# Output projection of a decoder block in seven block products, its weight differences made by adding transfers

## The chip, the cores and the metric

One core of a Trainium2 chip. The metric is the device time of one execution in microseconds, given as the median of three runs. The five engines (TensorE, VectorE, ScalarE, GpSimd or POOL, and SyncE, whose queue issues transfers) each work through a queue of their own in order and meet at semaphores.

## The reference, cut to what matters

One decoder layer for 512 tokens of width 1024, all in float32:

```python
p = x @ W_in + b_in                     # u, v, q, k, value, r, gate A, gate B
m = sigmoid(g_a) * y_a + sigmoid(g_b) * y_b     # y_a: spatial gating; y_b: gated linear attention * silu(r)
h = layer_norm(ALPHA * x + m @ W_out, ln1_g, ln1_b)
f = square(relu(h @ W_1)) @ W_2                 # 1024 -> 4096 -> 1024
out = layer_norm(ALPHA * h + f, ln2_g, ln2_b)
```

The change concerns `m @ W_out` (512 x 1024 by 1024 x 1024), the layer norm behind it, and the last gates ahead of it.

## The kernel before

**Split operands.** TensorE multiplies in a reduced float32 format (`F32R`). Each operand is split into an upper and a lower half: `split(hi, lo, src)` casts on ScalarE (L88) and subtracts on VectorE (L89). Each product is three passes: hi*hi, hi*lo, lo*hi.

**Weights.** All weights come as chunks of 128 x 1024 values (512 KB) in the order of the list `STREAM`. `load_to` issues the transfers on SyncE's queue into three `raw` buffers, `sum_to` makes weight differences on VectorE (L128), and `split_to` splits a chunk into `wh`, `wl`; there are `W_BUFS = 7` pairs of them, and a split is emitted up to seven chunks ahead of its use. One job of the gate stage uses one chunk (24 matmuls of 512 columns, 8 row blocks times three passes).

**Stages.** (1) Input projections, interleaved with the linear attention and the spatial gating. (2) The gate stage: `branch(e0)` takes the columns of r and of gate B in pairs, four jobs a pair; at the end tile `e` of `AT_` holds m transposed (128 channels x 512 tokens), and is split into `mh`, `ml`. (3) The output projection: two `row_unit`s, one for each half of the columns, four token tiles each, 24 matmuls a tile (L218). `out_take` adds ALPHA * x (L871), takes statistics (L872), and after the second half normalises the tile by rows (`ln_apply`: L638 to L646, with a power on POOL, L176). `turn_h` transposes a normalised tile on TensorE (L851, eight matmuls) and splits it into `xh`, `xl`, the right-hand operand of the feed-forward. (4) The feed-forward. Its first block is cut into two halves of 256 tokens (`hidden`), so that it can start when tiles 0 and 1 are there; tiles 2 and 3 are turned after its groups 0 and 2. Its second matrix is multiplied for three quarters of its rows in *seven products* instead of eight (`product_of`, Winograd's form of Strassen's scheme over 2 x 2 blocks): sums and differences of blocks on both sides, `GOES` and `accumulators` saying which PSUM banks a product adds to. The banks `x` carry products 1, 6, 7 and 4 in turn, the banks `v` products 5 and 3; each sum that is read out goes into a 128 x 512 quarter of the result.

**What sets the order.** Tensor, vector, scalar and POOL instructions stand in the order in which the code emits them. SyncE's queue is ordered by the scheduler. So an instruction that waits holds up all that was emitted behind it on its engine.

## Time and profile before

| | |
|---|---|
| median of three runs | 757.26 us (756.94 to 757.44) |
| the profiled execution | 757.19 us, span 755.4 us |
| granted TensorE clock | 0.998 |
| busy | PE 746.2, VectorE 473.8, ScalarE 343.6, POOL 29.8 us |
| transfers | 85.14 MB, 113 GB/s on average |

In the profile's rows, PE is TensorE's matmuls, PEld its weight loads, DVE is VectorE, ACT ScalarE, SP SyncE. A row of the timeline gives start and duration in us, engine, line and operation, `out<-in` by the program's names, and in brackets the idle time before it with what ended it. A row of the groups gives the count, then the busy time, the mean ns of one, and the idle time before. Matmuls overlap: one lasts 0.39 us in its row but the next starts sooner, so their cost is read from start to start.

### The profile page before, as it was taken

The numbers are of one execution on the slowest core, as the hardware profiler recorded it, in microseconds if no ns is written. First come the engines' busy times: TensorE is split into PE (matmuls) and PEld (weight loads), VectorE is DVE, ScalarE is ACT, GpSimd is POOL, SyncE is SP. The second block draws the span as 40 slices with busy tenths as digits, with TensorE's granted clock in tenths as the row PEclk, the third lists the DMA queues.
The fourth block names the chain that finished last, engine by engine and source line by source line (L and its number), as shares of the span: only waits on it lengthen the run. The fifth ranks groups of instructions, "written<-read, shape, count | busy, mean of one in ns | idle before, by whom it ended". The sixth has DMA issues, their size and how long they took to land.

```text
span 755.4 us, 8781 instructions
## 1 busy us (share of the span) xinstructions
PE 746.2 (99%) x3498; PEld 626.0 (83%) x3498; DVE 473.8 (63%) x592; ACT 343.6 (45%) x449; POOL 29.8 (4%) x60
## 2 busy tenths in 40 slices
PE   9999999999999999999999999999999999999996
PEld 7878888888888888888888988888888888888885
DVE  7478876676575554435458533777667856687655
ACT  7375744363254735444222544444444554455300
POOL 1000000000000102000002000000000000000001
PEclk9999999999999999999999999999999999999999
DMA  8533322222042132432240324145331734135111
GB/s 341 203 134 125 132 82 80 84 84 84 31 145 77 56 126 84 170 109 85 98 152 31 109 72 147 49 134 201 111 112 34 244 100 152 56 125 196 43 56 56
DMA packets 25464, 85.14 MB, mean 113 GB/s; under 512 B 3088, under 2 KB 3344, under 8 KB 25424
## 3 DMA queue, kind: packets, MB, share of 16 engines
q1 hardware_dynamic: 25280, 84.33, 32.3%
q8 instruction: 27, 0.44, 0.2%
q10 hardware_dynamic: 144, 0.26, 0.1%
q14 instruction: 13, 0.11, 0.0%
HBM read 82.48 MB, written 2.10 MB: 112 GB/s over the span
## 4 chain that ended last, share of the span: by engine, by line
PE 96%; issue 1%; DVE 1%; DMA 1%; POOL 0%; DVEq 0%; POOLq 0%
PE f L691 22%; PE ps L218 17%; PE mx L974 9%; PE f L1074 6%; PE gb L691 6%; PE r L691 6%; PE ga L691 6%; PE u L691 6%; PE mv L974 4%; PE qk L691 3%; PE first L275 3%; PE m L974 2%; PE sc L519 2%; PE pm L744 1%; PE po L553 1%
## 5 line engine op out<-in xcount | busy, mean ns | idle before, releaser
L89 DVE TENSOR_TENSOR wl<-raw,wh 128x1024 fp32r<-128x1024 f32 x141 | 171.1, 1222 | 114.4 <-ACT wh L88 112.6
L88 ACT CAST wh<-raw 128x1024 fp32r<-128x1024 f32 x141 | 145.7, 1044 | 48.7 <-PE ps L218 23.7
L691 PE MATMUL f<-xh,wh 128*128 128x512 f32 (+1 forms) x288 | 105.4, 366 | 0.0
L691 PE MATMUL f<-xl,wh 128*128 128x512 f32 (+1 forms) x288 | 105.3, 365 | 0.0
L691 PE MATMUL f<-xh,wl 128*128 128x512 f32 (+1 forms) x288 | 105.2, 365 | 0.0
L691 PEld LDWEIGHTS f<-xl,wh 128*128 128x128 f32 x288 | 54.3, 189 | 8.8
L691 PEld LDWEIGHTS f<-xh,wl 128*128 128x128 f32 x288 | 54.3, 189 | 8.7
L691 PEld LDWEIGHTS f<-xh,wh 128*128 128x128 f32 x288 | 54.3, 189 | 8.7
L914 ACT ACTIVATE F<-f 128x512 f32<-128x512 f32 (+1 forms) x28 | 15.0, 537 | 80.2 <-PE f L691 79.1
L218 PE MATMUL ps<-wh,xh 128*128 128x512 f32 x128 | 50.4, 394 | 0.0
L218 PE MATMUL ps<-wh,xl 128*128 128x512 f32 x128 | 49.8, 389 | 0.0
L218 PE MATMUL ps<-wl,xh 128*128 128x512 f32 x128 | 49.8, 389 | 0.0
L974 PE MATMUL mx<-wh,oh 128*128 128x512 f32 x96 | 37.3, 389 | 0.0
L974 PE MATMUL mx<-wl,oh 128*128 128x512 f32 x96 | 37.3, 389 | 0.0
L974 PE MATMUL mx<-wh,ol 128*128 128x512 f32 x96 | 37.3, 389 | 0.0
L128 DVE TENSOR_TENSOR raw<-raw,raw 128x1024 f32<-128x1024 f32 x24 | 29.2, 1218 | 2.6 <-DMA raw<-in_w_all 2.6
L218 PEld LDWEIGHTS ps<-wh,xl 128*128 128x128 f32 x128 | 24.0, 188 | 5.0
L218 PEld LDWEIGHTS ps<-wl,xh 128*128 128x128 f32 x128 | 24.0, 188 | 4.9
L218 PEld LDWEIGHTS ps<-wh,xh 128*128 128x128 f32 x128 | 24.0, 188 | 4.8
L691 PE MATMUL u<-xh,wh 128*128 128x512 f32 x64 | 25.9, 405 | 0.0
L691 PE MATMUL ga<-xh,wh 128*128 128x512 f32 x64 | 25.9, 404 | 0.0
L88 ACT CAST oh<-d 128x1024 fp32r<-128x1024 f32 x12 | 12.6, 1051 | 29.1 <-DVE d L947 29.1
(242 smaller groups left out, 1557.4 us busy)
## 6 DMA issues: line engine op xcount, KB each, us to landing
raw<-in_w_all SPq DMA_DIRECT2D x136, 512.0 KB, 3.4
bufB<-in_head SPq DMA_DIRECT2D x4, 512.0 KB, 8.0
xr<-in_x SPq DMA_DIRECT2D x8, 256.0 KB, 3.5
out<-bufA SPq DMA_DIRECT2D x8, 256.0 KB, 2.0
bufA<-in_head SPq DMA_DIRECT2D x3, 512.0 KB, 5.6
brow<-in_b_in SPq DMA_DIRECT2D x4, 256.0 KB, 6.2
g<-in_ln_g SPq DMA_DIRECT2D x2, 512.0 KB, 5.9
b<-in_ln_b SPq DMA_DIRECT2D x2, 512.0 KB, 5.5
```

What stands on the lines that cost most here:

```text
L88: nc.scalar.copy(hi, src)
L89: nc.vector.tensor_tensor(lo, src, hi.bitcast(F32), op=ALU.subtract)
L128: nc.vector.tensor_tensor(raw, x_, y_, op=ALU.subtract)
L218: nc.tensor.matmul(ps, s_, m_, start=(k == 0 and i == 0), stop=(k == KT - 1 and i == 2))
L275: nc.tensor.matmul(first[e], s_, m_[:, k, :], start=(k == 0 and i == 0), stop=(k == KT - 1 and i == 2))
L519: nc.tensor.matmul(sc[:, c, 0:192], pr.kt[:, jc * P : (jc + 1) * P], pr.qt[:, jc, :], start=True, stop=True)
L553: nc.tensor.matmul(po, pr.AT[:, j, c, :], vs, start=True, stop=(c == 0))
L691: nc.tensor.matmul(ps, s_, m_, start=(k == 0 and i == 0), stop=(k == KT - 1 and i == 2))
L744: nc.tensor.matmul(pm[:, c, :], bufB[:, c, gs], wst[:, g, :], start=True, stop=True)
L914: nc.scalar.activation(dst, ps, AF.Relu)
L974: nc.tensor.matmul(ps, s_, m_, start=(begins and k == 0 and i == 0), stop=(k == 3 and i == 2), skip_group_check=True,)
L1074: nc.tensor.matmul(ps, s_, m_, start=(f == 0 and i == 0), stop=(f == 7 and i == 2))
```

## The change

The output projection is done in seven products of 24 matmuls with 512 columns (`product_of`, moved up from the feed-forward), in the order 1, 2, 5, 6, 3, 7, 4. Its left operands are made in the gate stage: `as_it_is(k, m)` splits a block of m, `summed(k)` makes the four sums and differences on VectorE and splits them. The gate tiles are taken in the pairs `PAIRED`, so that block row k of both column blocks is there together. The weight differences aren't subtracted on VectorE: after the split of a chunk ScalarE negates it in place, and a transfer issued by POOL adds the next chunk from memory to it (eight times: chunks 56, 57, 60 to 65, whose sums become chunks 60 to 63 and 66 to 69).

The layer norm behind it is done in three ways. Tile 0: `rest_of_stats` and `normalise` (ScalarE, by a row's scale and bias, without gain and offset), the transposes, and then gain and offset by columns on ScalarE in PSUM; its rows get gain and offset later, in the second feed-forward block. Tiles 1, 2 and 3: by rows on VectorE as before, with the gain rows loaded into the buffers of product 1's operand.

```diff
+PAIRED = ((0, 1), (4, 5), (2, 6), (3, 7))
@@ split_to
             if raw is not None:
                 split(hi, lo, raw)
+            if i in NEXT_BY_DMA:
+                nc.scalar.mul(raw, raw, -1.0)
+                nc.gpsimd.dma_start(raw, w_all[STREAM[NEXT_BY_DMA[i]][4]], accum_op=ALU.add)
@@ product_of: also for the output projection
-                    split_to(u0 + k // 2 + 1 + W_BUFS)
+                    split_to(u0 + k // 2 + 1 + ahead)
@@ gate stage
-    for e in range(2, KT, 2):
-        branch(e)
+    def as_it_is(k, m):
+        e, i = {1: (k, 0), 2: (k + 4, 0), 4: (k + 4, 1)}[m]
+        hi, lo = mf if m == 1 else (mh[:, MADE[m]], ml[:, MADE[m]])
+        split(hi[:, k, :], lo[:, k, :], AT_[:, e, i * 256 : i * 256 + 256])
+    def summed(k):
+        a = lambda i, j: AT_[:, k + 4 * (j - 1), (i - 1) * 256 : i * 256]
+        d = [temp(f"ms{k}_{i}").rearrange("p (m t) -> p m t", m=2) for i in range(2)]
+        (s1, s2), (s4, s3) = [(x_[:, 0, :], x_[:, 1, :]) for x_ in d]
+        nc.vector.tensor_tensor(s1, a(2, 1), a(2, 2), op=ALU.add)
+        for o, x_, y_ in ((s2, s1, a(1, 1)), (s4, a(1, 2), s2), (s3, a(2, 1), a(1, 1))):
+            nc.vector.tensor_tensor(o, x_, y_, op=ALU.subtract)
+        for i in range(2):
+            split(mh[:, 2 * i : 2 * i + 2, k, :], ml[:, 2 * i : 2 * i + 2, k, :], d[i])
+    branch(PAIRED[1], {4: all_of(0), 5: all_of(1)})
+    branch(PAIRED[2], {6: all_of(2)})
+    branch(PAIRED[3], {3: all_of(3)[:1], 7: all_of(3)[1:]})
@@ output projection
-    row_unit(mh, ml, out_take(0))
-    at(S_O + 5, lambda: turn_h(0))
-    at(S_O + 6, lambda: turn_h(1))
-    row_unit(mh, ml, out_take(1))
+    def normalise(t):
+        row = bufA[:, t, :]
+        nc.scalar.activation(row, row, AF.Identity, bias=rs1[t][:, 1:2], scale=rs1[t][:, 0:1])
+    def turn_h(t):
...
+            for i in range(4 if t == 0 else 0):
+                e = half * 4 + i
+                g_, b_ = ln1c[:, e : e + 1], ln1c[:, 8 + e : 9 + e]
+                nc.scalar.activation(pt[:, i, :], pt[:, i, :], AF.Identity, bias=b_, scale=g_)
...
+    def project_take(m, t, ps):
+        i, j = GOES[m]
+        dst, tt = quarter(bufA, i, j)[:, t, :], 2 * i + t
+        if m in NEW:
+            xr = mpool.tile([P, 512], F32, name=f"xr{m}_{t}", tag="xr", bufs=2)
+            nc.sync.dma_start(xr, x[tt * P : (tt + 1) * P, j * 512 : j * 512 + 512])
+            nc.vector.scalar_tensor_tensor(dst, xr, ALPHA, ps, op0=ALU.mult, op1=ALU.add)
+        else:
+            nc.vector.tensor_add(dst, dst, ps)
+        if m in (2, 3, 7, 4):
+            stats(tt, j)
+        if m == 3 and t == 0:
+            rest_of_stats(0)
+        elif m in (3, 4):
+            if m == 3:
+                normalise(0)
+            st = st1[tt].rearrange("p a b -> p (a b)")
+            ln_apply(bufA[:, tt, :], bufA[:, tt, :], st, *rows1["gb"], lnp, f"l1{tt}")
+        if m == 7 and t == 0:
+            turn_h(0)
+        if m == 4:
+            if t == 0:
+                turn_h(1)
+    for m in ORDER:
+        ahead = {3: W_BUFS - 2, 7: W_BUFS - 2, 4: W_BUFS - 3}.get(m, W_BUFS)
+        product_of(f"o{m}", m, mf if m == 1 else (mh[:, MADE[m]], ml[:, MADE[m]]), project_take, ahead)
+        if m == 2:
+            rows1["gb"] = [row_bcast(mpool, a, D, f"mf{i}") for i, a in enumerate((ln1_g, ln1_b))]
@@ second feed-forward block, after its first job
+            nc.vector.tensor_mul(bufA[:, t, :], bufA[:, t, :], g1)
+            nc.vector.tensor_add(bufA[:, t, :], bufA[:, t, :], b1)
@@ the stream of chunks
+        if p < 0 and m in (5, 6, 7, 4):
+            place = {5: b(1, 2), 6: b(2, 2), 7: b(1, 2), 4: b(2, 1)}[m]
+            return (None, None, B if m == 7 else A, p, place)
+        if p < 0 and m == 3:
+            return (b(2, 2), B, B, p, None)
```

Three places of the queues follow. In the names, the number behind `wh`, `wl` or `raw` is the chunk, `mxo1_0` is a PSUM bank of the products (`x` bank, half 0), `mo2` one of product 2, `mvo5` a `v` bank, and `xr6_0` the x tile for product 6, half 0. In the rows before, `ps_60_2` is the PSUM bank of the second column half's token tile 2.

ScalarE, from the last gate job on, before:

```order
L815 ACTIVATE gb7_2809<-gb7_2784,cols_sb_101 128x512
L88 CAST wh62_2813<-raw62_2707 128x1024
L88 CAST mh_2359<-bufA_91 128x512
L88 CAST wh63_2920<-raw63_2745 128x1024
L88 CAST wh64_2932<-raw64_2780 128x1024
L88 CAST wh65_2944<-raw65_2817 128x1024
L88 CAST wh66_2960<-raw66_2924 128x1024
```

and now, from the casts of the last operand row on:

```order
L90 CAST mh_2357<-ms3_0_2859 128x2x256
L90 CAST mh_2357<-ms3_1_2860 128x2x256
L90 CAST mh_2357<-bufA_91 128x256
L90 CAST wh63_2899<-raw57_2441 128x1024
L154 ACTIVATE raw57_2441<-raw57_2441 128x1024
L90 CAST wh64_2911<-raw64_2743 128x1024
L154 ACTIVATE raw64_2743<-raw64_2743 128x1024
L90 CAST wh65_2942<-raw65_2783 128x1024
L154 ACTIVATE raw65_2783<-raw65_2783 128x1024
L90 CAST wh66_2956<-raw64_2743 128x1024
L90 CAST wh67_2991<-raw65_2783 128x1024
```

A negation (L154) stands between the casts of chunks 63, 64 and 65, and the casts of 66 and 67 read what the adding transfers leave.

VectorE, in the middle of the projection, before (first column half):

```order
L871 SCALAR_TENSOR_TENSOR bufA_91<-xr0_2_2909,ps_56_2_2884 128x512
L872 BN_STATS st1_2_2342<-bufA_91 128x6
L89 TENSOR_TENSOR wl63_2921<-raw63_2745,wh63_2920 128x1024
L89 TENSOR_TENSOR wl64_2933<-raw64_2780,wh64_2932 128x1024
L89 TENSOR_TENSOR wl65_2945<-raw65_2817,wh65_2944 128x1024
L871 SCALAR_TENSOR_TENSOR bufA_91<-xr0_3_2956,ps_56_3_2913 128x512
```

and now, from product 2 to product 6:

```order
L91 TENSOR_TENSOR wl65_2943<-raw65_2783,wh65_2942 128x1024
L91 TENSOR_TENSOR wl66_2957<-raw64_2743,wh66_2956 128x1024
L970 TENSOR_TENSOR bufA_91<-bufA_91,mo2_1_2921 128x512
L939 BN_STATS st1_1_2341<-bufA_91 128x6
L968 SCALAR_TENSOR_TENSOR bufA_91<-xr5_0_2982,mvo5_0_2968 128x512
L91 TENSOR_TENSOR wl67_2992<-raw65_2783,wh67_2991 128x1024
L91 TENSOR_TENSOR wl68_3004<-raw56_2439,wh68_3003 128x1024
L968 SCALAR_TENSOR_TENSOR bufA_91<-xr5_1_3007,mvo5_1_2969 128x512
L968 SCALAR_TENSOR_TENSOR bufA_91<-xr6_0_3022,mxo1_0_2876 128x512
L91 TENSOR_TENSOR wl69_3032<-raw57_2441,wh69_3031 128x1024
L91 TENSOR_TENSOR wl70_3042<-raw70_2948,wh70_3041 128x1024
L968 SCALAR_TENSOR_TENSOR bufA_91<-xr6_1_3047,mxo1_1_2877 128x512
```

The sums that free PSUM banks (L968, L970) now stand behind lower halves of weights that depend on the adding transfers.

VectorE, around the turn of tile 1, before:

```order
L640 SCALAR_TENSOR_TENSOR bufA_91<-bufA_91,mv_l11_3031,g1_2352 128x1024
L646 SCALAR_TENSOR_TENSOR bufA_91<-bufA_91,rs_l11_3032,b1_2354 128x1024
L89 TENSOR_TENSOR xl_90<-pturn_3038,xh_89 128x4x128
L89 TENSOR_TENSOR xl_90<-pturn_3045,xh_89 128x4x128
L871 SCALAR_TENSOR_TENSOR bufA_91<-xr1_2_3077,ps_60_2_3052 128x512
```

and now, from the statistics of tile 2 in product 4 on:

```order
L939 BN_STATS st1_2_2342<-bufA_91 128x6
L648 BN_AGGR mv_l12_3170<-st1_2_2342 128x2
L183 TENSOR_SCALAR rs_l12_3171<-mv_l12_3170 128x1
L650 SCALAR_TENSOR_TENSOR bufA_91<-bufA_91,mv_l12_3170,mf0_2964 128x1024
L656 SCALAR_TENSOR_TENSOR bufA_91<-bufA_91,rs_l12_3171,mf1_2966 128x1024
L91 TENSOR_TENSOR xl_90<-pturn_3177,xh_89 128x4x128
L91 TENSOR_TENSOR xl_90<-pturn_3184,xh_89 128x4x128
```

Before, the lower halves of a turned tile (`xl`) follow the normalisation of the tile after it (here tile 0's follow tile 1's, with a later projection unit still on TensorE). Now tile 1's follow the sum and the normalisation of tile 2, with half of product 4 and the feed-forward next on TensorE.

## Prediction

> **What bounds the kernel now.** I read the page's first lines, then the chain of waits in order of time, then the stretches (busy time by engine), then the rows of each engine around the output projection.

> ```profile
> span 755.4 us, 8781 instructions
> PE 746.2 (99%) x3498; PEld 626.0 (83%) x3498; DVE 473.8 (63%) x592; ACT 343.6 (45%) x449; POOL 29.8 (4%) x60
> GB/s 341 203 134 125 132 82 80 84 84 84 31 145 77 56 126 84 170 109 85 98 152 31 109 72 147 49 134 201 111 112 34 244 100 152 56 125 196 43 56 56
> ```
> TensorE (PE) is busy all the time; VectorE (DVE), ScalarE (ACT) and the transfers only matter where they make it wait.

> ```profile
> 268.00:368.00 100.00, 100.00 (x459) 83.07 (x458) 43.73 (x54) 46.31 (x71) 6.50 (x16) 1.00 0.33 113
> 368.00:420.00 52.00, 52.00 (x269) 44.50 (x268) 35.52 (x47) 13.39 (x18) 6.08 (x4) 1.00 0.32 107
> ```
> Columns: PE, weight loads, DVE, ACT, POOL, granted clock, DMA share, GB/s. In the gate stage (268 to 368) both helpers are under half busy. In the projection (368 to 420) VectorE already works 35.5 of 52 us, ScalarE 13.4.

> ```profile
> 367.49 32.64 PE ps L218 x144
> 400.13 0.87 PE pturn L851 x8
> 401.00 5.47 PE ps L218 x24
> 422.34 1.25 PE pturn L851 x8
> 423.59 47.06 PE f L691 x264
> ```
> Read off: 32.64/144 = 0.2267 us for a 512-column matmul, 0.87 us for one token tile's eight transposes. After 423.6 TensorE runs unbroken, so a shift at the start of the feed-forward carries to the end.

> ```profile
> 367.32 0.39 PE L218 MATMUL ps<-wh,mh 128*128 128x512 f32 x1
> 412.63 0.28 PE L691 MATMUL f<-xh,wh 128*128 128x256 f32 x1
> 426.51 0.38 ACT L914 ACTIVATE F<-f 128x256 f32<-128x256 f32 x1 [2.29 <-PE f L691]
> 429.39 0.38 ACT L914 ACTIVATE F<-f 128x256 f32<-128x256 f32 x1 [2.05 <-PE f L691]
> ```
> The window that changes starts with the first projection matmul (367.32) and ends with the fourth group of the half-width feed-forward, 0.2 us before its relu at 426.51: 426.3. Groups of 24 are 429.39 - 426.51 = 2.88 us apart. Work in the window: 192 x 0.2267 + 4 x 2.88 + 4 x 0.87 = 58.5 of 59.0 us; about 0.5 us is waiting.

> **The change, priced.** *Removed:* 24 of 192 matmuls, 5.44 us of TensorE. A product is then two halves of 2.72 us.

> *VectorE's prices in the window:*

> ```profile
> 406.50 0.69 DVE L871 SCALAR_TENSOR_TENSOR bufA<-xr,ps 128x512 f32<-128x512 f32 x1 [0.37 <-PE ps L218]
> 407.22 0.69 DVE L872 BATCH_NORM_STATS2 st<-bufA 128x6 f32<-128x512 f32 x1
> 407.95 0.21 DVE L638 BATCH_NORM_AGGREGATE mv_l<-st 128x2 f32<-128x12 f32 x1
> 408.20 0.16 DVE L173 TENSOR_SCALAR rs_l<-mv_l 128x1 f32<-128x1 f32 x1
> 408.27 1.28 DVE L640 SCALAR_TENSOR_TENSOR bufA<-bufA,mv_l,g 128x1024 f32<-128x1024 f32 x1
> 409.99 1.28 DVE L646 SCALAR_TENSOR_TENSOR bufA<-bufA,rs_l,b 128x1024 f32<-128x1024 f32 x1 [0.44 <-POOL rs_l L176]
> 411.19 1.28 DVE L89 TENSOR_TENSOR xl<-pturn,xh 128x512 fp32r<-128x512 f32 x2
> 412.39 3.48 DVE L89 TENSOR_TENSOR wl<-raw,wh 128x1024 fp32r<-128x1024 f32 x3
> 415.79 0.68 DVE L871 SCALAR_TENSOR_TENSOR bufA<-xr,ps 128x512 f32<-128x512 f32 x1
> 408.43 1.52 POOL L176 TENSOR_TENSOR rs_l<-rs_l,nhalf 128x1 f32<-128x1 f32 x1 [4.82 <-DVE rs_l L173]
> L176 POOL TENSOR_TENSOR ss<-ss,nhalf 128x1 f32<-128x1 f32 x16 | 8.8, 548 | 1.3
> ```
> From start to start: a sum out of PSUM 0.61 (0.72 if the next needs it), statistics 0.73, the rest of a tile's normalisation 3.24 (407.95 to 411.19), a lower half `xl` 0.60, a weight's lower half `wl` 1.13. The power on POOL takes 1.52 beside a VectorE operation with two SBUF operands, 0.55 elsewhere.

> *ScalarE's prices:*

> ```profile
> 367.52 0.69 ACT L815 ACTIVATE gb<-gb,cols_sb 128x512 f32<-128x512 f32 x1 [2.65 <-PE gb L691]
> 385.25 1.05 ACT L88 CAST wh<-raw 128x1024 fp32r<-128x1024 f32 x1 [14.93 <-PE ps L218]
> L450 ACT ACTIVATE kt<-kt 128x1024 f32<-128x1024 f32 x6 | 6.4, 1062 | 9.1 <-DVE kt L436 9.1
> L673 ACT ACTIVATE bufB<-bufB,rs_sg 128x1024 f32<-128x1024 f32 x4 | 4.9, 1232 | 0.0
> L290 ACT CAST als<-als 128x128 fp32r<-128x128 f32 x2 | 0.5, 296 | 0.0
> L580 ACT ACTIVATE bufB<-po,ss 128x256 f32<-128x256 f32 x16 | 6.8, 471 | 0.2 <-POOL ss L176 0.2
> L480 DVE TENSOR_TENSOR dr<-dr,k 128x256 f32<-128x256 f32 x4 | 1.7, 425 | 0.1
> ```
> A negation costs 1.06 (the 128x1024 activation with a constant scale), the row normalisation of tile 0 1.23. A 128x128 scaling by columns has no row: between 0.30 (a cast of that size) and 0.47 (256 columns with a scale column); 0.37 taken, in the middle, as both differ by one step. Now ScalarE idles 14.9 us before 385.25; that room goes.

> *Operands in the gate stage:* per row of blocks four 128x256 sums (0.43), two splits of 128x512 and three of 128x256 replace two of 128x512. That is about 3 us more of VectorE for each of four rows, beside 56 us idle in 268 to 368, and four PSUM banks let TensorE run ahead: nothing. Only the last row can show: its first operand is done at 367.2 and wanted at 369.4, its second at 372.7 and wanted at 374.8. Without that cover the first products wait. The new order of the gate tiles moves whole 5.44 us jobs: nothing.

> *Negations and adding transfers.* Eight negations on ScalarE, each waiting for VectorE's `wl` of the same chunk with later casts queued behind; eight transfers on POOL's queue, where only the powers stand behind them, later. The first two (wanted 20 us after issue) are free. The adding transfer is in no row.

> ```profile
> raw<-in_w_all SPq DMA_DIRECT2D x136, 512.0 KB, 3.4
> bufB<-in_head SPq DMA_DIRECT2D x4, 512.0 KB, 8.0
> DMA to landing us min/median/max: 2.5/3.5/4.9
> ```
> The last row is that of the x tiles. The adding transfer moves the same 512 KB and takes in the held 512 KB: 3.4 if the second stream is hidden, 3.4 + 512 KB at the page's best 341 GB/s (1.5) if not. Nearest is the plain chunk: I take 4.1; ends 3.4 and 8.0 (four heads queued). [...]

> *The path, step by step.* Last gate sigmoid 367.52; cast of chunk 62; VectorE multiplies, adds, makes its `wl` (370.8); negation to 371.9; ScalarE's casts of the last operand row follow, to 375.2. Then three rounds cast, `wl`, negation for 63, 64, 65, 1.05 + 1.22 + 1.06 + 0.2 each: negation of 64 ends 382.2, of 65 385.6. Their transfers land 386.3 and 389.7, and chunks 66 and 67 are cast behind them. Behind `wl66` stand, in VectorE's queue, two sums and a statistics; `wl67`, `wl68`, two sums, `wl69`, `wl70` and a sum follow, and only then the sums of product 3.
> 1. Product 3 (ideally 389.1) reuses the bank of product 5, whose first sum is read at 390.6: 1.6; its second half 0.4.
> 2. VectorE has idled 2.2 behind negation 63, 3.1 behind transfer 64, 0.5 for an x tile (3.5 us; SyncE's queue has two weight loads ahead of the second), and 0.5 in small gaps. So the first sum of product 3, ready at 392.2 on an undisturbed TensorE, starts at 398.0. Sum, statistics, aggregate: 399.8; POOL 0.55 + 0.27; ScalarE 1.23: tile 0 is normal at 402.0, transposes wanted at 399.2: 2.8. The 0.55 is taken because the next VectorE operation there reads PSUM; 1.52 would make this 3.8. [...]
> 3. VectorE normalises tile 1 by rows (to 404.5), product 7's first sum and statistics (405.8), tile 0's two `xl` behind eight scalings (8 x 0.41) and two casts (408.2), `wl71`, `wl72` (410.9), then the second sum of product 7 (411.5). The second half of product 4 adds into that bank and is wanted at 409.3: 2.2.
> 4. Statistics, then tile 2's sum and whole normalisation stand ahead of tile 1's `xl` in the queue: 417.5. The second matmul of the feed-forward wants it at 414.3: 3.2.

> Hidden: x tiles are eight before and after; gain and bias rows loaded once more (1 MB, DMA busy 0.32); tile 0's later multiply and add, 2.5 us of VectorE beside groups of 5.44 on TensorE. Cover gone: they would come on top.

> **Sum:** -5.44 + (1.6 + 0.4 + 2.8 + 2.2 + 3.2 = 10.2) - 0.5 (the waiting that is there now) = +4.3. The profiled execution took 757.19 us (755.4 span and 1.8 around it), 0.07 under the median: 761.5.

> **The rivals.** (a) *Faster.* If VectorE never idles behind negations and transfers, its queue has 15.7 us of work from 376.0 and reaches product 3's sum at 391.7, on time. From 392.2 it still has 18.1 us in a row before tile 1's first `xl` (410.3), wanted at 407.3, so 3.1 wait: -5.44 + 3.1 - 0.5 = -2.8, 754.4; without any wait 751.3. For it: VectorE idles 16 of 52 us now. Against it: the queue is in order, and a negation stands in front of the cast that VectorE needs. It decides at product 3's first sum: every microsecond it is late goes to the end one for one, and past 2.8 us late the kernel is slower. (b) *The adding transfer is slow.* Each microsecond over 4.1 adds one: 7 gives 764.4, 8.0 765.4, past 8.3 two for one, as two transfers then follow each other; 9 gives 767. For it: POOL makes this transfer, no row shows it; against: 0.32 busy share. (c) *They cancel:* half the lateness, within 1.5 us of 757.2. For it: my small gaps are rounded; against: the tail alone takes 3.1.

> **How the numbers follow.** A difference under 0.2% (1.5 us) can't be told from none. The forecast as worked out: 0.50; its own range goes from 759.3 (transfer 3.4, x tile 2.5, scaling 0.30) to 764.5 (x tile 4.9, scaling 0.47). Rival (b), above that: 0.12. Rival (c): 0.12. Rival (a): 0.26. Faster 0.26, same 0.12, slower 0.62. The range 753.5 to 766.5 takes in most of (a) and of (b) and leaves out some 0.07 below and 0.06 above.

> **What would show it.** Right: gaps on TensorE before product 3, before the transposes of tile 0 (released by ScalarE), before the second half of product 4 and at the second feed-forward matmul (both by VectorE), near 10 us in all; `wl66` and `wl67` waiting for casts that wait for the adding transfers; landing near 4 us. Wrong: TensorE without gaps between 389 and 418, VectorE at product 3's first sum by 394, or a wait in the gate stage or after 430, where I have none.

## The result, and the profile after

The changed kernel takes 767.35 us (median of 5 runs, 765.80 to 768.99), the kernel before 757.13 beside it (5 runs, 756.94 to 757.44): 1.0136 times as long, 95% interval 1.0123 to 1.0149. Slower was forecast, but by 4.3 us; it is 10.2, and 767.35 lies outside the range of 753.5 to 766.5.

The page of the changed kernel (its execution took 767.35 us), the lines that answer to those of before:

```profile
span 765.6 us, 8831 instructions
PE 745.0 (97%) x3474; PEld 624.7 (82%) x3474; DVE 494.4 (65%) x632; ACT 365.7 (48%) x484; POOL 36.1 (5%) x69
q0 software_dynamic: 1152, 4.19, 3.2%
raw<-in_w_all SPq DMA_DIRECT2D x134, 512.0 KB, 3.3
raw<-in_w_all POOLq DMA_DIRECT2D x8, 512.0 KB, 5.9
```

TensorE is 20.6 us short of the span; before it was 9.2. The last row is the adding transfer, 5.9 us in the median; q0 is POOL's queue (packets, MB, share of 16 engines). The same stretches as before, with the columns of the prediction's table:

```profile
268.00:368.00 100.00, 100.00 (x459) 83.11 (x458) 51.24 (x75) 53.38 (x85) 10.17 (x20) 1.00 0.35 106
368.00:420.00 52.00, 42.07 (x183) 33.77 (x181) 36.82 (x53) 24.42 (x34) 7.35 (x8) 0.93 0.66 172
```

In the gate stage the 7.5 us more of VectorE stay hidden. In the projection TensorE works 42.1 of 52 us, and the granted clock is no longer 1.00. TensorE's waits between 370 and 430 (engine, line, for whom; us in total, times, longest):

```profile
PE mvo L841 <- DVE bufA L968: 4.9, 1, 4.9
PE f L701 <- DVE xl L91: 2.8, 1, 2.8
PE mxo L841 <- DVE bufA L970: 2.0, 1, 2.0
PE pturn L954 <- ACT bufA L946: 1.9, 1, 1.9
```

These are the four places of the prediction. TensorE's rows at the first and the last:

```profile
394.00 0.76 PE L841 MATMUL mvo<-wh,mh 128*128 128x512 f32 x1 [4.92 <-DVE bufA L968]
394.57 0.63 PE L841 MATMUL mvo<-wl,mh 128*128 128x512 f32 x1
394.99 0.63 PE L841 MATMUL mvo<-wh,ml 128*128 128x512 f32 x1
395.42 0.63 PE L841 MATMUL mvo<-wh,mh 128*128 128x512 f32 x1
...
418.64 0.28 PE L701 MATMUL f<-xh,wh 128*128 128x256 f32 x1
421.76 0.39 PE L701 MATMUL f<-xl,wh 128*128 128x256 f32 x1 [2.85 <-DVE xl L91]
...
422.35 0.41 PE L701 MATMUL f<-xl,wh 128*128 128x256 f32 x1
422.57 0.41 PE L701 MATMUL f<-xh,wl 128*128 128x256 f32 x1
422.78 0.41 PE L701 MATMUL f<-xh,wh 128*128 128x256 f32 x1
```

Behind both gaps the matmuls come 0.427 us apart (394.99 to 395.42) instead of 0.227, and 0.213 instead of 0.12 in the half-width groups. TensorE's clock in stretches (busy, clock, DMA share, GB/s):

```profile
394.00:398.00 4.00, 4.00 (x10) 0.50 0.74 264
...
421.70:425.30 3.60, 3.54 (x17) 0.55 0.22 55
425.30:430.00 4.70, 4.70 (x42) 0.98 0.99 323
```

Ten matmuls at half speed cost 2.0 us, the seventeen and their neighbours 1.6. From start to start, less a matmul (or the transposes), the gaps are 5.07, 2.06, 2.19 and 3.00. The account of TensorE's time: the matmuls saved, the four gaps, the slow matmuls, less the waiting of before: -5.44 + 12.3 + 3.6 - 0.5 = +10.0, against 10.2 measured.

Where VectorE got late: the chain's steps of the transfer that makes chunk 66 from 64 and of the last x tile ahead of product 3's first sum; ScalarE's cast behind the first, then VectorE, at `wl66` and at that x tile:

```profile
382.21 7.36 DMA raw<-in_w_all
...
396.75 4.65 DMA xr<-in_x
```
```profile
389.64 1.04 ACT L90 CAST wh<-raw 128x1024 fp32r<-128x1024 f32 x1 [4.43 <-DMA raw<-in_w_all]
...
390.72 1.22 DVE L91 TENSOR_TENSOR wl<-raw,wh 128x1024 fp32r<-128x1024 f32 x1 [6.60 <-ACT wh L90]
...
401.50 0.69 DVE L968 SCALAR_TENSOR_TENSOR bufA<-xr,mxo 128x512 f32<-128x512 f32 x1 [1.57 <-DMA xr<-in_x]
402.10 0.68 DVE L970 TENSOR_TENSOR bufA<-bufA,mvo 128x512 f32<-128x512 f32 x1
```

The x tile is requested only when product 5's second sum (396.05 to 396.7) has freed one of the two `xr` buffers. So the last thing that product 3's first sum waits for is this transfer of 4.65 us, and it is so in the rows of the runs below, but for `plain_sp`'s, which name TensorE; no run changed the number of these buffers or the time of the request.

### The profile page after: what moved, and what is told of

Its sections match the earlier page's. It is cut to its first block, busy times and chain, and to the rows that moved or that the text cites. A ratio compares the mean times of both kernels' runs of the same rounds, so it can differ in the third digit from the quotient of the medians.

```text
span 765.6 us, 8831 instructions
## 1 busy us (share of the span) xinstructions
PE 745.0 (97%) x3474; PEld 624.7 (82%) x3474; DVE 494.4 (65%) x632; ACT 365.7 (48%) x484; POOL 36.1 (5%) x69
## 4 chain that ended last, share of the span: by engine, by line
PE 92%; DVE 3%; DMA 2%; issue 2%; ACT 1%; POOL 0%; DVEq 0%; POOLq 0%; ACTq 0%
PE f L701 23%; PE ps L228 11%; PE mx L841 9%; PE f L1137 6%; PE gb L701 6%; PE r L701 6%; PE ga L701 6%; PE u L701 6%; PE mv L841 4%; PE first L285 3%; PE qk L701 3%; PE m L841 2%; PE sc L529 2%; DMA raw<-in_w_all 1%; PE pm L754 1%
## 5 line engine op out<-in xcount | busy, mean ns | idle before, releaser
L91 DVE TENSOR_TENSOR wl<-raw,wh 128x1024 fp32r<-128x1024 f32 x147 | 178.3, 1223 | 118.8 <-ACT wh L90 117.2
L90 ACT CAST wh<-raw 128x1024 fp32r<-128x1024 f32 x147 | 151.3, 1043 | 31.3 <-DMA raw<-in_w_all 10.5
## 6 DMA issues: line engine op xcount, KB each, us to landing
raw<-in_w_all SPq DMA_DIRECT2D x134, 512.0 KB, 3.3
raw<-in_w_all POOLq DMA_DIRECT2D x8, 512.0 KB, 5.9
bufB<-in_head SPq DMA_DIRECT2D x4, 512.0 KB, 8.1
bufA<-in_head SPq DMA_DIRECT2D x3, 512.0 KB, 5.5
g<-in_ln_g SPq DMA_DIRECT2D x2, 512.0 KB, 6.1
```

Of the source, the lines that this page charges most:

```text
L90: nc.scalar.copy(hi, src)
L91: nc.vector.tensor_tensor(lo, src, hi.bitcast(F32), op=ALU.subtract)
```

## The experiments

**Theory T:** each gap is a loss of its own; the late transfers open the first, and gaps halve the clock. **Theory V:** VectorE's queue, in order, sets the start of the feed-forward; a gap or a slow stretch ahead of its next late operation costs nothing more. A rival to both: the order of the tail (tile 1's `xl` behind tile 2's normalisation) is the main cost.

### Why the adding transfer is slow

`plain_pool`: the adding taken out, all else kept.

```diff
-                nc.gpsimd.dma_start(raw, w_all[...], accum_op=ALU.add)
+                nc.gpsimd.dma_start(raw, w_all[...])
```

> POOL's eight transfers write over the held chunk instead of adding to it (the weight differences are left out; negations, queue and bytes are the same). If the adding makes them slow (accumulate): landing near the plain 3.3 us, gap before product 3 down by 3 to 4 us to 1 to 2, its clock loss gone: 761 to 763 us. If it is POOL's queue or other transfers beside them: landing stays at 6 to 7.5 us, 766 to 768 us.

765.01 us. The page, POOL's transfers and TensorE's waits:

```profile
q0 software_dynamic: 1152, 4.19, 1.6%
raw<-in_w_all POOLq DMA_DIRECT2D x8, 512.0 KB, 3.6
```
```profile
PE pturn L954 <- ACT bufA L946: 3.5, 1, 3.5
PE f L701 <- DVE xl L91: 2.9, 1, 2.9
PE mvo L841 <- DVE bufA L968: 1.6, 1, 1.6
PE mxo L841 <- DVE bufA L970: 1.0, 1, 1.0
```

It is the adding: with the same packets and bytes the 16 engines are busy for 1.6% of the span instead of 3.2%, 1.5 us a transfer instead of 3.1 (765.6 x 0.032 / 8). The eight land after 3.4, 3.6 and 4.0 us (least, median, most) against 5.0, 5.9 and 9.2. In the changed kernel the four early ones land after 5.0 to 5.6, the one requested at 372.03, beside the gain and bias rows, after 9.2, and the three late ones after 6.1, 7.4 and 6.5. But the time fell by 2.3, not by 4 to 6: the gap before product 3 shrank by 3.3, the one before the transposes grew by 1.6.

`rows`: the request of the gain and bias rows stands later in the program.

```diff
-        if m == 2:
+        if m == 5:
             rows1["gb"] = [...]
```

> The gain and bias rows (1 MB, 5.8 and 8.9 us) are requested after product 5 in the program instead of after product 2, so that they no longer move beside the adding transfers of chunks 66 and 67. If the sharing of the DMA engines makes these slow: they land in 4 to 5 us, the gap before product 3 falls to 2 to 3 us, its clock loss goes in part: 762 to 765 us. If the transfer is slow by itself: 7.4 and 6.6 us as before, 766 to 768 us. If the rows now land too late for tile 1's normalisation, that shows as VectorE waiting for mf, and the time rises.

766.11 us, but nothing moved: SyncE, whose queue the scheduler orders, requests the rows at 373.09, 5.41 us behind the projection's first matmul, and in the changed kernel at 372.57, 5.41 behind it too. So this is the changed kernel once more. It says nothing of the rows, and shows that two medians of one order of work can lie 1.2 us apart. What the changed kernel's trace shows: both rows (5.8 and 8.9 us) have landed by 381.9, before the deciding transfer is requested at 382.21, so they don't share the engines with it; whether they push back the adding transfers ahead of it stays open. In the changed kernel:

```profile
378.00:384.00 6.00, 6.00 (x28) 4.95 (x28) 4.22 (x5) 3.56 (x4) 1.75 (x2) 1.00 1.04 272
384.00:389.00 5.00, 5.00 (x23) 3.88 (x21) 0.12 (x1) 1.06 (x1) 0.88 (x1) 1.00 1.00 188
```

The DMA share (last but one) is full, at 188 GB/s: three adding transfers, 3.3 us apart, need 3.1 us of all engines each. In `plain_pool`, with the same rows and x tiles beside it, the share is 0.60 in both stretches. In `rows` and `sub6` this transfer landed after 7.38 and 7.45 us. What it costs isn't fixed: in `late_d4`, which makes it too, product 3 waited 3.3 us instead of 4.9.

`sub6` was meant to take away the late pair; the expectation names the wrong chunks. Product 6 uses 62 and 63, made early, and the late ones, 66 and 67, are product 7's. So it is the control for the early pair:

```diff
-        if p < 0 and m in (5, 6, 7, 4):
+        if p < 0 and m in (5, 7, 4):
...
-        if p < 0 and m == 3:
-            return (b(2, 2), B, B, p, None)
```

> Product 6's two differences (chunks 66 and 67) are made on VectorE from a chunk loaded in the ordinary way; the other six stay negations with adding transfers. Theory T (the late adding transfers of 66 and 67, 7.4 and 6.6 us, hold ScalarE's and then VectorE's queue; the gap before product 3 follows from them, and TensorE's halved clock follows from that gap): the gap of 5.07 us before product 3 and its 2.0 us of clock loss go, the gap of 2.06 before tile 0's transposes shrinks to 0 to 1, the tail's gap stays or grows by 0 to 2: 757 to 760 us. Rival R2 (VectorE is too full for its queue whatever the transfers do, and gets 2.4 us more work here): product 3 still waits 3 us or more, 765 us or above.

767.27 us: to make the early pair's differences on VectorE instead gains nothing, which fits the prediction's nothing for them. `sub7` takes away the right pair (and its subtraction is b(1,2) less b(2,2), made by VectorE):

```diff
+        if p < 0 and m == 7:
+            return (b(1, 2), None, B, p, (None, B))
```

> Product 7's two differences (chunks 66 and 67, made from 64 and 65; the ones whose transfers took 7.4 and 6.6 us) are made on VectorE from plainly loaded chunks; their two negations and adding transfers go, the other six stay. Theory T (every microsecond by which those transfers are late goes to the end): gap before product 3 under 1 us, its clock loss gone, no other gap grows: 757 to 760 us. Theory V (VectorE's own queue, in order, sets the end of the stage; the late transfer only puts idle time into it): gap before product 3 under 1, but the sum of product 3 still comes at 397 to 399 instead of 402, and the gap before tile 0's transposes grows to 3.5 to 4.5 with a clock loss behind it: 763 to 765 us.

763.43 us, as V said. TensorE's waits:

```profile
PE pturn L954 <- ACT bufA L946: 4.7, 1, 4.7
PE f L701 <- DVE xl L91: 2.9, 1, 2.9
PE mxo L841 <- DVE bufA L970: 0.5, 1, 0.5
PE mvo L841 <- DVE bufA L968: 0.4, 1, 0.4
```

4.5 us of gap went before product 3, and 2.8 came back before the transposes, since product 3's first sum came at 398.36; VectorE waited 2.5 us for its x tile there.

### What a gap is worth

`plain_sp`: no differences at all.

```diff
+        if p < 0:
+            return ({1: b(1, 1), 2: b(2, 1), 5: b(1, 2), 6: b(2, 2), ...}[m], None, None, None, None)
```

> All fourteen chunks of the projection's weights are loaded in the ordinary way by SyncE; there are no negations, no adding transfers and no differences of weights (these are left out). The prediction's rival (a) in pure form: VectorE never idles behind them. By its sum 754.4, with a clock loss of 1.5 behind a tail gap of 3 us 755 to 757 us: no gap before product 3, transposes' gap under 1.5. If VectorE's other work alone is too much for the stage: product 3's first sum after 396, transposes' gap over 2, 760 us or more.

759.65 us, between the two. Product 3's first sum comes at 395.57, by estimate behind an x tile: VectorE frees its buffer at 390.20 and reads it at 394.97, 4.77 us later, as at 396.73 and 401.50 in the changed kernel. Three waits stay:

```profile
PE pturn L954 <- ACT bufA L946: 2.1, 1, 2.1
PE mxo L841 <- DVE bufA L970: 2.0, 1, 2.0
PE f L701 <- DVE xl L91: 1.3, 1, 1.3
```

So the waits from product 3's sum on are 5.4 us, as much as the matmuls save, even with no weight difference. `fill3`, `fillf` and `fill` put matmuls that nothing reads into the gaps:

```diff
+        if m == 3:
+            fill(20)
...
+    def fill(n):          # into a bank that nothing reads
+        for i in range(n):
+            nc.tensor.matmul(ps, mh[:, 2, 0, 0:P], ml[:, 2:4, 0, :], start=True, stop=True)
...
+            if part == e == 0:
+                for _ in range(20):
+                    nc.tensor.matmul(ps[:, :256], hh[:, 0, 0:P], hh[:, 0, 0:256], start=True, stop=True)
```

> 20 matmuls of 512 columns into a spare PSUM bank stand before product 3 and 20 of 256 columns before the first feed-forward group: 4.5 and 2.4 us of work that nothing reads, inside the gaps of 5.07 and 3.0. If the halved clock comes from the gap, both halved stretches go. If the clock loss adds to the end wherever it lies (theory T): 2.0 and 1.55 less, 763.5 to 764 us. If VectorE's queue sets the transposes' time (theory V), the 2.0 turn into a longer gap there (2.1 to about 4) and only the last 1.55 are gained: 765.5 to 766 us. If the clock does not depend on the gap: half-speed rows stay, 767 us.

> Only the 20 matmuls of 512 columns before product 3 (4.5 us inside the gap of 5.07), nothing else changed. If the clock loss behind that gap (2.0 us) adds to the end: 765.3 us. By theory V the transposes wait for a sum that VectorE makes at 402 either way: the 2.0 become a longer gap there and the time stays at 766.5 to 768 us.

> Only the 20 matmuls of 256 columns before the first feed-forward group (2.4 us inside the gap of 3.0). No wait follows there, so by both theories the slow matmuls behind it (1.55 us) are a loss of their own: 765.5 to 766.2 us. If the time stays at 767.3, the clock loss is not on the path there either and the missing microseconds are elsewhere.

764.70, 767.69 and 765.22 us. Before product 3 nothing is gained, as V says: the slow matmuls of product 3 went, and the wait for the transposes grew from 1.9 to 4.1. Before the feed-forward 2.1 us are gained in the median, of runs from 763.76 to 767.29; the profiled execution is the slowest of them and shows no gain, since there the filling held the second matmul up by 1.0 us. Both together gain 2.65.

```profile
PE pturn L954 <- ACT bufA L946: 4.1, 1, 4.1
PE f L701 <- DVE xl L91: 2.9, 1, 2.9
PE mxo L841 <- DVE bufA L970: 0.4, 1, 0.4
```

These are `fill3`'s waits. What V says is then seen across all the kernels that keep the order of the tail. Starts in each profiled execution: VectorE's first sum of product 3, the second feed-forward matmul, their difference, and the rest of the span behind it:

| kernel | sum | matmul | difference | rest |
|---|---|---|---|---|
| changed | 402.10 | 421.76 | 19.66 | 343.84 |
| rows | 402.78 | 422.44 | 19.66 | 342.36 |
| sub6 | 403.19 | 422.84 | 19.65 | 342.36 |
| plain_pool | 398.87 | 418.97 | 20.10 | 343.83 |
| sub7 | 398.36 | 418.46 | 20.10 | 342.74 |
| fill | 400.92 | 421.04 | 20.12 | 342.36 |
| fill3 | 401.67 | 421.33 | 19.66 | 345.07 |
| fillf | 402.66 | 423.28 | 20.62 | 342.22 |
| subpool | 395.97 | 416.06 | 20.09 | 343.94 |
| plain_sp | 395.57 | 415.22 | 19.65 | 342.68 |

The sum moves over 7.6 us, the difference over 0.5, but for `fillf`, where the filling itself comes in between. The rest is 342.2 to 342.7 with the clock full behind the last gap, 343.8 to 343.9 with half speed for 3.4 us there, and 345.07 with half speed for 6.8 us (`fill3`).

`tail`: tile 1's lower halves ahead of tile 2's normalisation.

```diff
+        if m == 4 and t == 0:
+            turn_h(1)
         if m in (2, 3, 7, 4):
             stats(tt, j)
...
-        if m == 4:
-            if t == 0:
-                turn_h(1)
```

> Tile 1's transposes' lower halves (xl) stand ahead of tile 2's normalisation in VectorE's queue; nothing else moves. Theory T: the gap of 3.0 us at the second feed-forward matmul goes to under 0.5, and its clock loss of 1.55 with it, while tile 2's transposes may wait about 1: 763 to 764 us; the gap before product 3 stays at 5. Rival R1 (this order is the main cost of the change): 757 us or less. If the clock loss doesn't follow from the gap: 764 to 765 us with half-speed matmuls still after the start of the feed-forward.

762.89 us, 4.5 less, just under the 763 to 764 expected. The wait at the feed-forward and the slow matmuls behind it are gone, one of 0.5 at tile 2's transposes came. The rival that this order is the main cost asked for 757 or less from this move alone.

### Other ways to make the differences, and other orders

`subpool`: all eight differences subtracted on POOL, from plainly loaded chunks.

```diff
-                    nc.vector.tensor_tensor(raw, x_, y_, op=ALU.subtract)
+                    (nc.gpsimd if STREAM[i][3] < 0 else nc.vector).tensor_tensor(raw, x_, y_, op=ALU.subtract)
...
-        if p < 0 and m in (5, 6, 7, 4):
+        if p < 0 and m == 7:
+            return (b(1, 2), None, B, p, (None, B))
+        if False:
```

> All eight differences of the projection's weights are subtracted on POOL, which idles there, from plainly loaded chunks; no negations and no adding transfers. No run shows the price of a 128x1024 subtraction on POOL; VectorE's takes 1.22 us, and POOL's power took 1.52 instead of 0.55 beside a VectorE operation with two SBUF operands. If POOL gets each done in under 3 us and does not slow VectorE: as the kernel without differences, 755 to 759 us. If it waits for VectorE or slows it: the casts of chunks 66 and 67 wait for POOL, 760 to 767 us.

761.73 us. POOL's subtractions, and VectorE's two `wl` beside them, which take 2.8 us each instead of 1.2:

```profile
L135 POOL TENSOR_TENSOR raw<-raw,raw x4: 2401/2899/3397, 377.5 to 386.8; 128x1024 f32<-128x1024 f32 x4
```
```profile
385.59 5.66 DVE L91 TENSOR_TENSOR wl<-raw,wh 128x1024 fp32r<-128x1024 f32 x2 [1.47 <-ACT wh L90]
```

Even so product 3's first sum comes at 395.97, 6.1 earlier. `late_d` and `late_p` make the move of `tail` and put tile 0's transposes behind the whole of product 7, with adding transfers and with POOL's differences:

```diff
-        if m == 7 and t == 0:
+        if m == 7 and t == 1:
             turn_h(0)
```

> Adding transfers stay as changed. Tile 1's lower halves stand ahead of tile 2's normalisation (762.89 alone), and tile 0's transposes now stand behind the whole of product 7 instead of its first half, so the sum of its second half is ahead of tile 0's lower halves on VectorE. Theory T (each gap is a loss of its own): the gaps of 2.3 at the transposes and of 2.2 before product 4's second half go, nothing takes their place: 758 to 759 us. Theory V (VectorE's queue from product 3's first sum to tile 1's lower halves is about 16 us of work and sets the start of the feed-forward): both gaps go, and one of 3 to 4 us with a halved clock behind it comes back at the second feed-forward matmul: 761.5 to 763.5 us.

> The eight differences are subtracted on POOL (761.73 alone), and the two moves of the run beside it are made. By theory V the first sum of product 3 comes at 396, tile 1's lower halves 16 us behind it at 412, wanted at 407.5: one gap of 4 to 5 us before the feed-forward and 1.5 of halved clock: 757 to 759 us. By theory T 753 to 755 us.

760.75 and 756.35 us, both better than V said and worse than T said. `late_p` is the only kernel that isn't slower than before: 0.9990 times as long (0.9981 to 0.9999, 11 runs), less than the 0.2% that count. Its waits:

```profile
PE mxo L841 <- DVE bufA L970: 1.9, 1, 1.9
PE pturn L954 <- ACT bufA L946: 0.4, 1, 0.4
```

The wait at the feed-forward that V had put there didn't come: with the sums ahead VectorE no longer idles for tile 0's casts, and tile 1's lower halves begin 13.1 us behind product 3's first sum (396.27 to 409.40), not 16. Between the two kernels lie 4.4 us, the price in this order of the adding transfers over POOL's subtractions. The two moves alone take 6.6 us off the changed kernel, POOL's subtractions alone 5.6, both together 11.0: order and transfers weigh about the same, so the rival of the tail's order is half right once tile 0's transposes are moved too. More tries to shorten VectorE's queue:

```diff
@@ late_p2: tile 2 as tile 0
+        elif m == 4 and t == 0:
+            rest_of_stats(2)
+            normalise(2)
...
-            for i in range(4 if t == 0 else 0):
+            for i in range(4 if t % 2 == 0 else 0):
@@ late_p3: that, and
-        ahead = {3: W_BUFS - 2, 7: W_BUFS - 2, 4: W_BUFS - 3}
+        ahead = {3: W_BUFS - 2, 7: W_BUFS - 4, 4: W_BUFS - 3}
...
             turn_h(1)
+            split_to(73)
@@ late_p4: the edit of late_p3 without that of late_p2, and; late_d4: the same with adding transfers
+        if m == 4 or (m == 7 and t == 1):
+            tt = tt if m == 4 else 1
...
-            elif e in (0, 2):
-                turn_h(2 + e // 2)
+            elif e in (1, 2):
+                turn_h(1 + e)
```

> As the run with POOL's differences and both moves, and tile 2 is normalised as tile 0 is (mean and scale on ScalarE before the transposes, gain and bias by columns behind them, its row multiply and add later beside the feed-forward): 2.6 us less of VectorE behind tile 1's lower halves. By theory V the gap before the feed-forward stays and only a wait of tile 2's transposes goes: 0.5 to 1.5 us less than that run.

> As the run with tile 2 on ScalarE, and the splits of chunks 71 and 72 (two lower halves of 1.13 us on VectorE) stand behind tile 1's lower halves instead of ahead. By theory V these come 2.3 us earlier and the gap before the feed-forward falls to about 2 us, too short for the clock to fall: 753.5 to 756 us, faster than both kernels. If VectorE's queue is not the bound there: no difference to the run with tile 2 on ScalarE.

> POOL's differences and both moves (756.35), and VectorE's order is changed again: both sums of product 7 stand ahead of tile 1's normalisation, the lower halves of chunks 71 and 72 behind tile 1's, and the transposes of tiles 2 and 3 come one and one half-width group later. By theory V the gap of 2.1 before product 4 goes, 1 to 3 us of small waits remain at the feed-forward's start: 753.5 to 756 us. If each wait only moves on: 756 to 757 us.

> The same order as that kernel with the eight negations and adding transfers of the change. What is left between the two is what the adding transfers cost once the order behind them is repaired: product 3's first sum at 401 instead of 396, so 4 to 5 us more, 758 to 761 us. If the order was all that mattered: within 1.5 us of the kernel with POOL's differences.

761.64, 763.63, 758.00 and 763.40 us: four misses; of the last the difference comes near (5.4 us for the adding transfers, 4 to 5 expected). `late_p4` lost the wait before product 4 for which it was made and got another; in `late_p2` and `late_p3` the wait at the feed-forward that they were to leave or to shorten was not there, and tile 3's transposes began to wait. The 2 us that `late_p3`'s expectation calls too short for the clock to fall are those of the changed kernel, where gaps of 2.06 and 2.19 left it at 1.00; in `late_p` it fell behind one of 2.13 (400.44 to 403.44, less the transposes). In `late_p2` tile 2's columns, scaled in PSUM on ScalarE (1.8 us and a cast for each bank, by the rows of `late_p3`), hold the banks that tile 3's transposes want; in `late_p4` tile 3's wait for tile 2's split. One line of each, `late_p2` first:

```profile
PE pturn L954 <- DVE xl L91: 3.7, 2, 2.0
```
```profile
PE pturn L954 <- DVE xl L91: 2.9, 1, 2.9
```

## Why the prediction was wrong

Right: the direction; the place and the releaser of each of the four gaps; the last three gaps' sizes within 0.8 us (2.06, 2.19, 3.00 against 2.8, 2.2, 3.2; the 2.06 in part by luck, as VectorE was 4.1 us later there than predicted and TensorE 5.1, by 3.1 more of the first gap and 2.0 of slow matmuls); the early transfers and the gate stage at nothing; the negation's price (1.06); the power's 0.55 in tile 0's chain (0.56 beside a sum out of PSUM, and 1.51 for tile 1's beside a VectorE operation with two SBUF operands, begun 0.16 us ahead of it). In the kernel before, two powers took 0.55 even though such an operation began beside them, 0.06 and 0.21 us behind their start (300.76 and 256.41). VectorE's queue from product 3's first sum to the second feed-forward matmul was worked out at 19.5 us and took 19.66.

Wrong, in three terms:
1. *The adding transfer*, taken at 4.1 from ends of 3.4 and 8.0. Issued at 382.21, when the prediction had the negation end (382.2), it landed after 7.36. The four early ones took 5.0 to 5.6, over the 4.9 that the prediction's estimate gives for a held chunk whose stream isn't hidden, and the three in a row, with the engines full (share 1.04 and 1.00), 6.1 to 7.4. The ends of 3.4 and 8.0 took it in, the value chosen between them was too low; rival (b), one microsecond for each over 4.1, gives 764.8 for it.
2. *The x tiles*: 0.5 predicted, 0.24 + 1.57 measured, 1.3 more. With both, product 3's first sum should come 4.6 late; it came at 402.10 instead of 398.0, 4.1.
3. *The clock*, which the prediction left out, and so put at nothing: half-speed matmuls cost 3.6 us, of which 2.0 are taken up by the next wait for VectorE (`fill3` gains nothing) and 1.6 count, as nothing waits behind them (the rest is 343.84 instead of 342.36).

With these the profiled execution comes to 761.5 + 4.1 + 1.6 = 767.2. `plain_pool`, where the deciding transfer took 4.03, is the prediction's own premise: it took 765.0, 3.5 over, of which 0.9 are a later sum, 0.6 a longer queue behind it (20.10) and 1.5 the clock; the rest lies between its profiled execution (764.6) and the median. So the transfer alone isn't the miss. One sum of the prediction doesn't come out either: its own range's upper end, 764.5, is 0.8 more than the two terms named for it give (1.4 and 8 x 0.10 over 761.5); a transfer of 4.9 would make that up.

Rival (a) said 754.4 if VectorE never idles behind negations and transfers. `plain_sp` is that and took 759.65. The rival's queue, which was to reach product 3's sum at 391.7, on time, reached it at 395.57, 3.4 after the 392.2 at which the prediction has its first half ready: by the same estimate the x tile again. Behind it come not one wait of 3.1 but three, 5.9 in all from start to start, and the queue to the second matmul is 19.65 instead of 18.1. The 3.4 and the 1.6 make up 5.0 of the 5.3 us. Its turning point (slower past 2.8 us late) put this kernel on the right side: it is 1.0036 times as long as before (1.0024 to 1.0049).

## What to carry to other kernels

When one engine's queue sets the end of a stage, follow its time to the next fixed point; a gap closed on the engine that waits came back here at the next place where it meets that queue (with `fill3` 1.9 us before the transposes became 4.1). An adding transfer kept the DMA engines busy twice as long as a plain one of the same bytes (3.1 us against 1.5), and three of them 3.3 us apart filled the engines and landed after 6.1 to 7.4 us instead of 5.0 to 5.6, though the pair wanted 20 us later cost nothing (`sub6`). Look in the trace whether an edit moved the request that it was to move. Half speed followed waits on TensorE of 1.9 (`late_p`) to 4.9 us here and didn't follow others of 1.9 and 2.0 (the changed kernel, before the transposes and product 4): after a predicted gap of that size price a stretch of half-speed matmuls (1.6 and 2.0 us here), and ask whether another wait comes before the end that takes it up.

## What the runs showed of the hardware

```profile
409.23 0.54 PE L841 MATMUL mxo<-wh,mh 128*128 128x512 f32 x1 [2.02 <-DVE bufA L970]
...
409.99 0.63 PE L841 MATMUL mxo<-wh,ml 128*128 128x512 f32 x1
410.42 0.63 PE L841 MATMUL mxo<-wh,mh 128*128 128x512 f32 x1
```

The two slow stretches of the changed kernel begin 30.72 us apart, nine times 3.413. In `fillf`, `late_p3`, `late_p2` and `late_d4` the edges of two slow stretches, read off the spacing of the matmuls, lie six, seven, eight and ten times 3.413 us apart, within 0.02 us. Cut along these edges into stretches of 3.413 us, the changed kernel's trace has 1.18 and 0.56 us of TensorE's work in the two ahead of half speed (387.91 and 418.63); its gap of 3.06 lies in two with 1.93 and 2.87, and full speed follows both. In `plain_sp` the stretch ahead of half speed holds 1.39, in `late_p` and `late_p2` 1.50; the least found ahead of full speed, in `late_p3` from 414.34 on, is 1.68. So in these profiles the work in the stretch ahead tells the two apart. What ends half speed isn't shown: a slow stretch with 2.74 us of work was followed by another in `late_d` (392.33 to 395.74), one with 2.73 by full speed in `late_d4` (426.23 to 429.64).

Where the slow stretches fall may be part of why the changed kernel's runs spread over 3.2 us and those of before over 0.5: the rest behind the last gap is 342.4 in some profiled executions and 343.8 in others. The wait before product 3, 3.3 us in `late_d4` and 4.9 here, may be another part. Where they fell in the runs that were not profiled isn't known.
